# Sums of the activations made in SBUF after a copy out of PSUM, and block loads of the weights issued by GpSimd, in a one-core decoder block

## The chip, the cores and the metric

The kernel runs on one core of a Trainium2 chip. The metric is the device time of one execution in microseconds (us). Below, PE is TensorE's matmul stream and PEld its weight loads, DVE is VectorE, ACT is ScalarE, POOL is GpSimd, and SP is SyncE, which in this kernel mostly issues DMAs.

## The reference

One decoder layer over 256 rows of 2048 numbers, in fp32. Three attention-like mixers are merged through gates, and then comes the part that the change touches, a feed-forward block of width 8192:

```python
x = x + merged @ w_out[layer]
h2 = _rms(x, g_ffn_norm[layer])
x = x + jnp.square(jax.nn.relu(h2 @ w_ff_in[layer])) @ w_ff_out[layer]
```

## The kernel before, in words

Every weight is read from HBM once, as fp32. A tile `raw` is split into `whi` (an ACT cast, L187) and `wlo = raw - whi` (DVE, L188), the activations are split the same way into a high and a low half, and each product is made of three matmul passes: high by `whi`, low by `whi`, high by `wlo`. One pass over one k-tile (128 of the 2048 rows of a weight) is a matmul of 128x128 by 128x512. `split_into` (ACT L275, DVE L276) does the same split for all other tiles.

The feed-forward block runs in four quarters of 2048 hidden columns. A quarter first makes its hidden rows (`w_ff_in`), then adds their product with `w_ff_out` to the output. From the second half of quarter 0's `w_ff_out` on, the work is done in **units** (`unit`, L281) of 1024 columns: one unit in quarter 0, four in each later quarter (two of `w_ff_in`, then two of `w_ff_out`), 13 in all. In a unit, six of the 16 k-tiles go through a seven-product scheme of Strassen's kind over a 2x2 grid of blocks (two halves of the rows, two halves of the columns, two groups of three k-tiles). The other ten k-tiles are plain items, marked `n`. The order of a unit is fixed:

```python
UNIT = _order("B11", "n", "n", "n", "T2", "n", "T3", "n", "T1", "n", "B21", "n", "B22", "n", "T4", "n", "n")
```

Each letter item comes in two pieces, a of two k-tiles and b of one (`SUBS`), an `n` item is two k-tiles. The scheme needs two kinds of sums:

- **Sums of weight blocks** (`uload`). The four blocks B12, B11, B21 and B22 of a unit are loaded as tiles `sraw` of 768 KB (`fetch`, L203). DVE forms T3 = B22 - B12 (L216), T2 = B11 + T3 (L218), T1 (L222) and T4 (L230), each 128x1536. L216 needs the fourth block, which is asked for last. `fetch` for the next unit is called one block at a time, after items T2, T3, T1 and B21 of the current one. Before the change SP issues these loads, in one queue with the loads of `raw`.
- **Sums of the activations' blocks** (`sums_of`): four sums of the high/low input, split and kept in `sx` (of the normed input `x1T`, made once, from the SBUF tiles `xs`) or in `ss` (of a quarter's hidden rows, once per quarter, so four times). They are made in two pieces, of two k-tiles and of one.

`hidden_rows` makes the hidden rows: for each half of the rows four PE transposes put the squared ReLU `y` into a PSUM bank `tp` (L794), ACT and DVE split it into `hid` (L275, L276), and, before the change, `sums_of` reads both `tp` banks for its sums. It is a generator: `pump()` advances the queue `posts` (these rows) and the queue `attn` (side work) by one step after each item. For quarters 1 to 3 the second piece of `sums_of` falls between item `n` and item T3 of the quarter's second `w_ff_in` unit.

PSUM has four banks `acc`, two banks `sc` and two banks `tp`. The products B11 and T2 accumulate in `sc` banks; T3 and T1 take the two `tp` banks (name `pp`), the same that the transposes use. Every engine works through its instructions in a fixed order, which the compiler's scheduler sets from the program's order and the queues; `wahead` keeps the split of three items' weights ahead of PE, with four buffers each of `raw`, `whi` and `wlo` and six of `sraw`.

Of the kernel before, what the change touches and what calls it, by code (L numbers as in the profile page):

```python
# [11 lines left out]
F32 = mybir.dt.float32  # L12
F32R = mybir.dt.float32r
AF = mybir.ActivationFunctionType
ALU = mybir.AluOpType
# [3 lines left out]
P = 128  # L19
# [26 lines left out]
SH = 3  # L46
K1, K2 = [0, 1, 4], [2, 3, 5]
SUBS = [(0, 2), (2, 1)]
# [46 lines left out]
def tile_block(ctx: ExitStack, tc: tile.TileContext, io):  # L95
    nc = tc.nc
# [29 lines left out]
    posts, attn = deque(), deque()  # L126

    def step(queue):
        try:
            next(queue[0][1])  # L130
        except StopIteration:
            queue.popleft()
# [6 lines left out]
    def drain(queue, label):  # L139
        while any(l == label for l, _ in queue):  # L140
            step(queue)
# [26 lines left out]
    last_load = [None]  # L168
# [24 lines left out]
    def fetch(u, n):  # L193

        if u == len(units):
            return
        name, at = units[u]
        size = P * SH * 512
        got = ready.setdefault(u, {})
        for i, k in enumerate(list(BLOCKS)[len(got):n], len(got)):  # L200
            off = (at * len(BLOCKS) + i) * size
            got[k] = pool[0].tile([P, SH, 512], F32, tag="sraw", name="sraw")
            last_load[0] = nc.sync.dma_start(  # L203
                got[k], io[name][off:off + size].rearrange("(p g n) -> p g n", p=P, g=SH)).ins

    def uload(name, which):

# [64 lines left out]
    def split_into(hi, lo, src, scale=None):  # L272

        if scale is None:
            nc.scalar.copy(hi, src)  # L275
            nc.vector.tensor_tensor(lo, src, hi.bitcast(F32), op=ALU.subtract)  # L276
        else:
            nc.scalar.activation(hi, src, AF.Copy, scale=scale)  # L278
            nc.vector.scalar_tensor_tensor(lo, src, scale, hi.bitcast(F32), op0=ALU.mult, op1=ALU.subtract)

    def unit(name, sums, xh, xl, early, late):  # L281


# [359 lines left out]
    for t in range(2):  # L643
        nc.vector.scalar_tensor_tensor(zf[:, t, :], acc[t][:, 256:260], rstd[:, t:t + 1], bf,
                                       op0=ALU.mult, op1=ALU.add)
# [71 lines left out]
    ff = ctx.enter_context(tc.tile_pool(name="ff", bufs=1))  # L717
# [4 lines left out]
    for c in range(4):  # L722
# [6 lines left out]
        for j in range(2):  # L729
            tp = ps_tp.tile([P, 2, S], F32, tag="tp", name="tp")  # L730
# [18 lines left out]

    x1h, x1l = rows_of(x1T)  # L750

    S_USE = {"T1": 0, "T2": 1, "T3": 2, "B22": 3}

    def sums_of(a, ss):

        (a11, a12), (a21, a22) = a
        n = ss.shape[3]
        sf = ff.tile([P, 4, n, P], F32, tag="sf", name="sf", bufs=1)
        a21s = ff.tile([P, n, P], F32, tag="a21", name="a21s", bufs=1)
        nc.scalar.copy(a21s, a21)  # L760
        nc.vector.tensor_tensor(sf[:, 0], a22, a21s, op=ALU.add)  # L761
        nc.vector.tensor_tensor(sf[:, 2], a11, a21s, op=ALU.subtract)
        nc.vector.scalar_tensor_tensor(sf[:, 1], a11, -1.0, sf[:, 0], op0=ALU.mult, op1=ALU.add)
        nc.vector.tensor_tensor(sf[:, 3], a12, sf[:, 1], op=ALU.subtract)
        split_into(ss[:, 0], ss[:, 1], sf)

    def sums_for(at, ss):

        sums = {k: (lambda hl, g, i=i: ss[:, hl, i, g, :]) for k, i in S_USE.items()}
        sums["B11"] = lambda hl, g: at(K1[g], hl, slice(0, P))  # L770
# [4 lines left out]
    def partial_sums(p1, p6, p7, p5):  # L775
        p1s = ff.tile([P, 512], F32, tag="p1", name="p1s", bufs=1)
        uu = ff.tile([P, 2, 512], F32, tag="uu", name="uu", bufs=1)
        wz = ff.tile([P, 2, 512], F32, tag="wz", name="wz", bufs=1)
        nc.scalar.copy(p1s, p1)
        nc.vector.tensor_tensor(uu[:, 0, :], p6, p1s, op=ALU.add)  # L780
        nc.vector.tensor_tensor(uu[:, 1, :], p7, uu[:, 0, :], op=ALU.add)
        nc.vector.tensor_tensor(wz, p5[:, None, :].to_broadcast([P, 2, 512]), uu, op=ALU.add)
        return p1s, uu[:, 1, :], wz

    def hidden_rows(ys, hh, ss, wait):

        for _ in range(wait):
            yield
        tps = []
        for t in range(2):  # L790
            yield
            tp = ps_tp.tile([P, 4, P], F32, tag="tp", name="tp")
            for i in range(4):
                nc.tensor.transpose(tp[:, i, :], ys[t][:, i * P:(i + 1) * P], ident)  # L794
            ts = slice(t * P, (t + 1) * P)
            split_into(hh[:, :, 0, ts], hh[:, :, 1, ts], tp)
            tps.append(tp)
        if ss is not None:
            yield
            g0, n = SUBS[ss[1]]  # L800
            sums_of([[tp[:, n * i:n * i + n, :] for i in range(2)] for tp in tps], ss[0][:, :, :, g0:g0 + n, :])


    rrow = ff.tile([P, S], F32, name="rrow")
    sx = ff.tile([P, 2, 4, SH, P], F32R, name="sx")
# [16 lines left out]
            scaled.append(f)  # L822

    def split_rows():
        yield
        for g, f in enumerate(scaled):
            yield
            split_into(x1T[:, 4 * g:4 * g + 4, 0, :], x1T[:, 4 * g:4 * g + 4, 1, :], f)
            if g < len(SUBS):
                yield  # L830
                g0, n = SUBS[g]
                sums_of([[f[:, n * j:n * j + n, i * P:(i + 1) * P] for j in range(2)] for i in range(2)],
                        sx[:, :, :, g0:g0 + n, :])

    for q in range(4):
        hid = [ff.tile([P, 4, 2, S], F32R, tag="hid", name="hid", bufs=4) for _ in range(4)]
        ss = ff.tile([P, 2, 4, SH, P], F32R, tag="ss", name="ss", bufs=1)
        for sidx in range(4 if q == 0 else 0):
            if sidx == 1:
                attn.append(("x", scale_rows()))  # L840
            acc = strip_rows("w_ff_in", 512, KT, x1h, x1l)
            ys = []
            for t in range(2):
                y = ff.tile([P, 512], F32, tag="y", name="y", bufs=4)
                nc.scalar.activation(y, acc[t], AF.Relu, scale=ss2[:, t:t + 1])
                nc.scalar.activation(y, y, AF.Square)
                ys.append(y)
            posts.append(("h", hidden_rows(ys, hid[sidx], (ss, sidx) if sidx < len(SUBS) else None, 1)))
        for u in range(2 if q else 0):
            more = {}  # L850

            def early(*p):
                more[0, 0], more[0, 1], wz = partial_sums(*p)
                more[1, 0], more[1, 1] = wz[:, 0, :], wz[:, 1, :]

            def late(c, t, acc):
                y = ff.tile([P, 512], F32, tag="y", name="y", bufs=4)
                nc.vector.tensor_tensor(y, acc, more[c, t], op=ALU.add)
                nc.scalar.activation(y, y, AF.Relu)
                nc.scalar.activation(y, y, AF.Square)  # L860
                more["y", t] = y
                if t:
                    i = 2 * u + c
                    posts.append(("h", hidden_rows([more["y", 0], y], hid[i], (ss, i) if i < len(SUBS) else None,
                                                   0 if c else 2)))

            unit("w_ff_in", sums_for(lambda kt, hl, ts: x1T[:, kt, hl, ts], sx), x1h, x1l, early, late)
        if q == 0:
            drain(attn, "x")
            attn.append(("x", split_rows()))  # L870
        hidh = lambda kt, t: hid[kt // 4][:, kt % 4, 0, t * P:(t + 1) * P]
        hidl = lambda kt, t: hid[kt // 4][:, kt % 4, 1, t * P:(t + 1) * P]
        for c in range(0 if q else 2):
            acc = strip_rows("w_ff_out", 512, KT, hidh, hidl)
            cs = slice(c * 512, (c + 1) * 512)
            for t in range(2):
                nc.vector.tensor_tensor(x1[:, t, cs], acc[t], x1[:, t, cs], op=ALU.add)
        for u in range(0 if q else 1, 2):
            cols = [slice(1024 * u + 512 * c, 1024 * u + 512 * (c + 1)) for c in range(2)]

            def early(*p):
                p1s, u3, wz = partial_sums(*p)
                nc.vector.tensor_tensor(x1[:, 0, cols[0]], p1s, x1[:, 0, cols[0]], op=ALU.add)
                nc.vector.tensor_tensor(x1[:, 1, cols[0]], u3, x1[:, 1, cols[0]], op=ALU.add)
                nc.vector.tensor_tensor(x1[:, :, cols[1]], wz, x1[:, :, cols[1]], op=ALU.add)

            def late(c, t, acc):
                nc.vector.tensor_tensor(x1[:, t, cols[c]], acc, x1[:, t, cols[c]], op=ALU.add)  # L888
                if q == 3:
                    load(io["out"][t * P:(t + 1) * P, cols[c]], x1[:, t, cols[c]])  # L890

            unit("w_ff_out", sums_for(lambda kt, hl, ts: hid[kt // 4][:, kt % 4, hl, ts], ss), hidh, hidl, early, late)
        drain(attn, "x")
# [71 lines left out]
```

## Time and profile before

| | |
|---|---|
| time, median of 3 runs | 1412.69 us (1409.19, 1413.38, 1412.69) |
| profiled execution, its own time | 1411.21 us |
| span of the profiled execution (first to last instruction) | 1409.4 us |
| mean granted TensorE clock | 0.997 of 2.4 GHz |
| PE busy | 1393.0 us (99%) |
| DVE, ACT, POOL busy | 1024.9 us (73%), 759.9 us (54%), 37.5 us (3%) |
| HBM read | 271.31 MB, 194 GB/s over the span |

The profile is of one execution. Busy time counts the instructions of an engine; a matmul's end is modelled, and waits are put down to the last thing that was released. The span leaves out 1.8 us of the execution's own time.

### The profile page before, as it was taken

The page shows a single profiled execution, that of the slowest core. Times are in us where ns is not written, and L with a number is a line of the kernel's source. Part 1 is how long each engine was busy: PE and PEld are TensorE (multiplying, and loading weights), DVE is VectorE, ACT ScalarE, POOL GpSimd, SP SyncE. Part 2 cuts the span into 40 slices and gives each one's busy share as a digit, 9 for nine tenths or more (in the row PEclk, how much of TensorE's full clock was granted, in tenths as well). Part 3 has the DMA queues.
Part 4 walks back from the last instruction along what each step waited for, and adds up shares of the span by engine and source line. Part 5 has one row for each costly group of instructions (what it writes and reads, how often), then busy time and mean ns, then how long its engine had stood idle before and what let it go on. Part 6 is the DMA issues. An engine that isn't in the chain of part 4 may idle for free.

```text
span 1409.4 us, 17262 instructions
## 1 busy us (share of the span) xinstructions
PE 1393.0 (99%) x6343; PEld 1153.1 (82%) x6343; DVE 1024.9 (73%) x1167; ACT 759.9 (54%) x983; POOL 37.5 (3%) x41
## 2 busy tenths in 40 slices
PE   8999999999999999999999999999999999999998
PEld 6888888888888888888888888878888788887887
DVE  6647657566755646565567758899988899988996
ACT  7545545466444444444455635566555665556653
POOL 0211102000000000000000000000000000000000
PEclk9999999999999999999999999999999999999999
DMA  9747555655566666676675755655666556665562
GB/s 326 239 139 239 169 148 165 197 184 165 182 207 198 199 200 200 196 233 204 183 231 180 228 188 185 219 186 176 200 210 198 172 184 206 207 191 181 187 207 77
DMA packets 75524, 274.54 MB, mean 195 GB/s; under 512 B 8624, under 2 KB 9392, under 8 KB 75184
## 3 DMA queue, kind: packets, MB, share of 16 engines
q1 hardware_dynamic: 75296, 273.42, 60.6%
q8 instruction: 50, 0.82, 0.2%
q14 instruction: 34, 0.28, 0.1%
q10 hardware_dynamic: 144, 0.02, 0.0%
HBM read 271.31 MB, written 2.10 MB: 194 GB/s over the span
## 4 chain that ended last, share of the span: by engine, by line
PE 73%; DVE 0%; ACT 0%; issue 0%
PE acc L265 33%; PE acc L292 31%; PE pp L292 8%; PE tp L794 1%; PE tp L734 0%; PE tp L706 0%; DVE hid L276 0%; ACT hid L275 0%; DVE sf L761 0%; ACT a21s L760 0%; DVE x L888 0%; PE rr L813 0%
## 5 line engine op out<-in xcount | busy, mean ns | idle before, releaser
L188 DVE TENSOR_TENSOR wlo<-raw,whi 128x1024 fp32r<-128x1024 f32 (+2 forms) x425 | 509.6, 1204 | 283.1 <-ACT whi L187 274.2
L187 ACT CAST whi<-raw 128x1024 fp32r<-128x1024 f32 (+2 forms) x425 | 441.3, 1039 | 455.9 <-PE acc L265 313.7
L265 PE MATMUL acc<-whi,xT 128*128 128x512 f32 (+1 forms) x1472 | 393.6, 389 | 5.7 <-ACT xT L278 5.4
L265 PEld LDWEIGHTS acc<-whi,xT 128*128 128x128 f32 x1472 | 272.7, 189 | 61.5 <-ACT xT L278 6.1
L265 PE MATMUL acc<-wlo,xT 128*128 128x512 f32 (+1 forms) x736 | 226.2, 388 | 0.0
L275 ACT CAST whi<-sraw 128x1024 fp32r<-128x1024 f32 (+1 forms) x182 | 151.0, 837 | 115.3 <-PE acc L292 83.4
L276 DVE TENSOR_TENSOR wlo<-sraw,whi 128x1024 fp32r<-128x1024 f32 (+1 forms) x182 | 169.8, 953 | 22.2 <-ACT whi L275 16.4
L292 PE MATMUL acc<-whi,hid 128*128 128x512 f32 x644 | 166.4, 391 | 0.0
L265 PEld LDWEIGHTS acc<-wlo,xT 128*128 128x128 f32 x736 | 136.9, 188 | 28.1 <-issue 1.0
L292 PE MATMUL acc<-whi,x1T 128*128 128x512 f32 x552 | 140.7, 391 | 0.0
L292 PEld LDWEIGHTS acc<-whi,hid 128*128 128x128 f32 x644 | 120.3, 188 | 24.5
L292 PEld LDWEIGHTS acc<-whi,x1T 128*128 128x128 f32 x552 | 103.2, 188 | 21.2
L292 PE MATMUL acc<-wlo,hid 128*128 128x512 f32 x322 | 91.1, 390 | 0.0
L292 PE MATMUL acc<-wlo,x1T 128*128 128x512 f32 x276 | 76.9, 390 | 0.0
L292 PEld LDWEIGHTS acc<-wlo,hid 128*128 128x128 f32 x322 | 60.2, 188 | 12.4
L265 PE MATMUL acc<-whi,x1T 128*128 128x512 f32 x256 | 70.0, 394 | 0.0
L265 PE MATMUL acc<-whi,mT 128*128 128x512 f32 x256 | 69.9, 392 | 0.0
L265 PE MATMUL acc<-whi,oT 128*128 128x512 f32 x224 | 60.0, 390 | 0.6 <-ACT oT L278 0.6
L292 PEld LDWEIGHTS acc<-wlo,x1T 128*128 128x128 f32 x276 | 51.6, 188 | 10.6
L265 PEld LDWEIGHTS acc<-whi,mT 128*128 128x128 f32 x256 | 47.9, 188 | 9.6
L265 PEld LDWEIGHTS acc<-whi,x1T 128*128 128x128 f32 x256 | 47.5, 188 | 9.4
L265 PEld LDWEIGHTS acc<-whi,oT 128*128 128x128 f32 x224 | 42.0, 188 | 9.6 <-ACT oT L278 0.9
(201 smaller groups left out, 1337.5 us busy)
## 6 DMA issues: line engine op xcount, KB each, us to landing
raw<-in_w_gate_dram SPq DMA_DIRECT2D x96, 512.0 KB, 3.6
raw<-in_w_ff_in_dram SPq DMA_DIRECT2D x92, 512.0 KB, 4.1
raw<-in_w_ff_out_dram SPq DMA_DIRECT2D x86, 512.0 KB, 4.3
raw<-in_w_proj_dram SPq DMA_DIRECT2D x77, 512.0 KB, 3.9
sraw<-in_w_ff_out_blocks_dram SPq DMA_DIRECT2D x28, 768.0 KB, 4.5
sraw<-in_w_ff_in_blocks_dram SPq DMA_DIRECT2D x24, 768.0 KB, 5.5
raw<-in_w_out_dram SPq DMA_DIRECT2D x32, 512.0 KB, 3.5
raw<-in_w_up_c_dram SPq DMA_DIRECT2D x12, 512.0 KB, 3.5
```

Source lines behind the costliest of these rows:

```text
L187: nc.scalar.copy(hi[:, gs, :], raw[:, gs, :])
L188: nc.vector.tensor_tensor(lo[:, gs, :], raw[:, gs, :], hi[:, gs, :].bitcast(F32), op=ALU.subtract)
L265: nc.tensor.matmul(acc[t][:, :n], lhsT=xs(kt, t), rhs=ws[:, g, :], start=(first and kt == 0), stop=(last and kt == nkt - 1),)
L275: nc.scalar.copy(hi, src)
L276: nc.vector.tensor_tensor(lo, src, hi.bitcast(F32), op=ALU.subtract)
L292: nc.tensor.matmul(acc, lhsT=x(hl, g), rhs=w[:, g, :], start=(first and i == 0 and g == 0), stop=(last and i == 2 and g == n - 1))
L794: nc.tensor.transpose(tp[:, i, :], ys[t][:, i * P:(i + 1) * P], ident)
```

## The change

Two edits, and a third that follows from them.

1. The block loads in `fetch` are issued by GpSimd in place of SP, and no longer note themselves as the last load (to which later small loads are tied).
2. The activations' blocks are copied out of PSUM by ACT right after the transposes (`keep`, into a tile `sf` of SBUF), and `sums_of` becomes a step by step generator that runs later, in the `attn` queue, in place in `sf`, for all three k-tiles at once. The copy `a21s` and the scalar form of the second sum are gone. `drain(attn, "s")` makes sure that the sums are written before the quarter's `w_ff_out` starts.
3. `hidden_rows` is a step shorter for the rows that carry sums, so what follows it in `posts` comes a step earlier, and the scheduler's order moves around it.

```diff
@@ fetch
             got[k] = pool[0].tile([P, SH, 512], F32, tag="sraw", name="sraw")
-            last_load[0] = nc.sync.dma_start(
-                got[k], io[name][off:off + size].rearrange("(p g n) -> p g n", p=P, g=SH)).ins
+            nc.gpsimd.dma_start(got[k], io[name][off:off + size].rearrange("(p g n) -> p g n", p=P, g=SH))
@@ sums
-    S_USE = {"T1": 0, "T2": 1, "T3": 2, "B22": 3}
-
-    def sums_of(a, ss):
-
-        (a11, a12), (a21, a22) = a
-        n = ss.shape[3]
-        sf = ff.tile([P, 4, n, P], F32, tag="sf", name="sf", bufs=1)
-        a21s = ff.tile([P, n, P], F32, tag="a21", name="a21s", bufs=1)
-        nc.scalar.copy(a21s, a21)
-        nc.vector.tensor_tensor(sf[:, 0], a22, a21s, op=ALU.add)
-        nc.vector.tensor_tensor(sf[:, 2], a11, a21s, op=ALU.subtract)
-        nc.vector.scalar_tensor_tensor(sf[:, 1], a11, -1.0, sf[:, 0], op0=ALU.mult, op1=ALU.add)
-        nc.vector.tensor_tensor(sf[:, 3], a12, sf[:, 1], op=ALU.subtract)
-        split_into(ss[:, 0], ss[:, 1], sf)
+    S_USE = {"T3": 0, "T2": 1, "T1": 2, "B22": 3}
+
+    def sums_of(sf, ss):
+
+        def op(dst, a, b, how):
+            nc.vector.tensor_tensor(sf[:, dst], sf[:, a], sf[:, b], op=how)
+
+        yield
+        op(2, 0, 2, ALU.add)
+        op(0, 1, 0, ALU.subtract)
+        yield
+        op(1, 2, 1, ALU.subtract)
+        op(3, 3, 1, ALU.subtract)
+        yield
+        nc.scalar.copy(ss[:, 0], sf)
+        yield
+        nc.vector.tensor_tensor(ss[:, 1], sf, ss[:, 0].bitcast(F32), op=ALU.subtract)
+
+    def keep(sf, i, t, src):
+
+        g0, n = SUBS[i]
+        nc.scalar.copy(sf[:, 1 - t::2, g0:g0 + n, :], src.rearrange("p (h g) n -> p h g n", h=2))
@@ hidden_rows
-            tps.append(tp)
-        if ss is not None:
-            yield
-            g0, n = SUBS[ss[1]]
-            sums_of([[tp[:, n * i:n * i + n, :] for i in range(2)] for tp in tps], ss[0][:, :, :, g0:g0 + n, :])
+            if sf is not None:
+                keep(sf[0], sf[1], t, tp[:, :2 * SUBS[sf[1]][1], :])
+                if t and sf[1] == len(SUBS) - 1:
+                    attn.append(("s", sums_of(sf[0], sf[2])))
@@ split_rows (the sums sx of the input)
             if g < len(SUBS):
-                yield
-                g0, n = SUBS[g]
-                sums_of([[f[:, n * j:n * j + n, i * P:(i + 1) * P] for j in range(2)] for i in range(2)],
-                        sx[:, :, :, g0:g0 + n, :])
+                for t in range(2):
+                    keep(sfx, g, t, f[:, :2 * SUBS[g][1], t * P:(t + 1) * P])
+        yield from sums_of(sfx, sx)
@@ loop over the quarters
             attn.append(("x", split_rows()))
+        drain(attn, "s")
```

How the order of instructions moves is shown at three places. In such rows a bracket lists the engines or queues that the instruction waits for (DMAHW a transfer issued by SP, DMASW one issued by GpSimd), and x3 stands for three more of the same.

PE, around item T3 of the second `w_ff_in` unit of quarters 1 to 3 (the same in all three). `tp<-ident,y` are the transposes of the second half of the hidden rows, `acc<-whi,x1T` and `acc<-wlo,x1T` plain matmuls, `pp<-whi,sx` the first product of T3. Before:

```order
L292 MATMUL acc<-whi,x1T 128x512 [waits Activation_49]
L292 MATMUL acc<-whi,x1T 128x512 x7
L292 MATMUL acc<-wlo,x1T 128x512 [waits DVE_49]
L292 MATMUL acc<-wlo,x1T 128x512 x3
L794 MATMUL tp<-ident,y 128x128 [waits DVE_49]
L794 MATMUL tp<-ident,y 128x128 x3
L292 MATMUL pp<-whi,sx 128x512 [waits DVE_49,PE_49]
```

and now:

```order
L800 MATMUL tp<-ident,y 128x128 [waits PE_49,Activation_49]
L800 MATMUL tp<-ident,y 128x128 x3
L291 MATMUL acc<-whi,x1T 128x512 [waits Activation_49]
L291 MATMUL acc<-whi,x1T 128x512 x7
L291 MATMUL acc<-wlo,x1T 128x512 [waits DVE_49]
L291 MATMUL acc<-wlo,x1T 128x512 x3
L291 MATMUL pp<-whi,sx 128x512 [waits PE_49,Activation_49]
```

The transposes stood right ahead of T3's first product; now twelve plain matmuls stand between them, and the product waits for ACT where it waited for DVE.

DVE, around the sum T3 = B22 - B12 of a unit (before L216, now L215; the place shown is the third unit). `wlo<-sraw,whi` is the low half of a block's piece, `wlo<-raw,whi` that of an `n` item, `wz<-pp,uu` belongs to the products. Before:

```order
L782 TENSOR_TENSOR wz<-pp,uu 128x1024 [waits DVE_49,PE_49]
L188 TENSOR_TENSOR wlo<-raw,whi 128x1024 [waits DMAHW6_49,Activation_49]
L276 TENSOR_TENSOR wlo<-sraw,whi 128x1024 [waits PE_49,Activation_49]
L216 TENSOR_TENSOR sraw<-sraw 128x1536 [waits DMAHW4_49,DMAHW1_49]
L276 TENSOR_TENSOR wlo<-sraw,whi 128x512 [waits PE_49,Activation_49]
L188 TENSOR_TENSOR wlo<-raw,whi 128x1024 [waits DMAHW7_49,PE_49,Activation_49]
L218 TENSOR_TENSOR sraw<-sraw 128x1536 [waits DMAHW0_49,DVE_49]
```

and now:

```order
L789 TENSOR_TENSOR wz<-pp,uu 128x1024 [waits DVE_49,PE_49]
L188 TENSOR_TENSOR wlo<-raw,whi 128x1024 [waits DMAHW5_49,Activation_49]
L275 TENSOR_TENSOR wlo<-sraw,whi 128x1024 [waits PE_49,Activation_49]
L275 TENSOR_TENSOR wlo<-sraw,whi 128x512 [waits PE_49,Activation_49]
L215 TENSOR_TENSOR sraw<-sraw 128x1536 [waits DMASW3_49,DMASW0_49]
L188 TENSOR_TENSOR wlo<-raw,whi 128x1024 [waits DMAHW6_49,PE_49,Activation_49]
L217 TENSOR_TENSOR sraw<-sraw 128x1536 [waits DMASW1_49,DVE_49]
```

The split of the 512-column piece went from behind the sum to ahead of it, and the sum waits for transfers issued by GpSimd.

PE, where the `w_ff_in` part of quarters 1 to 3 ends and `w_ff_out` begins. `pp<-whi,hid` and `acc<-whi,hid` are the first matmuls of `w_ff_out`; the transposes need the sums `y` of the last `acc<-wlo,x1T` passes (two matmuls each for the four pairs of column half and row half, the pair of the transposes shown first). Before:

```order
L292 MATMUL acc<-wlo,x1T 128x512 [waits DVE_49]
L292 MATMUL acc<-wlo,x1T 128x512 x3
L292 MATMUL pp<-whi,hid 128x512 [waits Activation_49]
L292 MATMUL pp<-whi,hid 128x512 x3
...
L292 MATMUL acc<-wlo,hid 128x512 [waits DVE_49]
L292 MATMUL acc<-wlo,hid 128x512 x3
L292 MATMUL acc<-whi,hid 128x512 [waits DVE_49,Activation_49]
L292 MATMUL acc<-whi,hid 128x512 x3
L794 MATMUL tp<-ident,y 128x128 [waits Activation_49]
```

and now:

```order
L291 MATMUL pp<-whi,hid 128x512 [waits Activation_49]
L291 MATMUL pp<-whi,hid 128x512 x3
L291 MATMUL acc<-wlo,x1T 128x512 [waits DVE_49]
L291 MATMUL acc<-wlo,x1T 128x512 x3
L291 MATMUL acc<-wlo,x1T 128x512 [waits DVE_49]
L291 MATMUL acc<-wlo,x1T 128x512 x3
L291 MATMUL pp<-wlo,hid 128x512 [waits DVE_49]
L291 MATMUL pp<-wlo,hid 128x512
L291 MATMUL pp<-whi,hid 128x512 [waits Activation_49]
...
L291 MATMUL acc<-whi,hid 128x512 [waits DVE_49,Activation_49]
L291 MATMUL acc<-whi,hid 128x512 x3
L800 MATMUL tp<-ident,y 128x128 [waits Activation_49]
```

Between the last matmul that the first transposes' `y` needs and the transposes stood 26 matmuls in quarters 2 and 3 (32 in quarter 1); now it is 15 in all three.

SP issues 52 loads fewer (its rows fall from 198 to 102), POOL issues these 52, all behind its last small operation.

## Rows read from the trace of the kernel before

**Rows 1.** Part 1 of the page, busy time of each engine.

```profile
PE 1393.0 (99%) x6343; PEld 1153.1 (82%) x6343; DVE 1024.9 (73%) x1167; ACT 759.9 (54%) x983; POOL 37.5 (3%) x41
```

**Rows 2.** Waits of PE: us in total, times, longest.

```profile
PE pp L292 <- DVE sf L761: 6.3, 3, 2.1
```

**Rows 3.** The chain of waits from 943.88: start us, us, what.

```profile
943.88 2.77 PE acc L292 x12
946.65 0.45 PE tp L794 x4
...
947.12 0.59 ACT hid L275
...
947.74 0.70 DVE hid L276
...
948.47 0.27 ACT a21s L760
...
948.76 0.30 DVE sf L761
```

**Rows 4.** Groups by line, forms together: count, busy us, mean ns, idle before.

```profile
L761 DVE TENSOR_TENSOR sf<-tp,a21s 128x256 f32<-128x256 f32 (+1 forms) x8 | 2.8, 354 | 1.3 <-ACT a21s L760 1.3
L276 DVE TENSOR_TENSOR ss<-sf,ss 128x1024 fp32r<-128x1024 f32 (+1 forms) x8 | 7.6, 952 | 2.1 <-ACT ss L275 2.1
L275 ACT CAST ss<-sf 128x1024 fp32r<-128x1024 f32 (+1 forms) x8 | 6.7, 834 | 3.2 <-DVE sf L764 3.2
```

**Rows 5.** Groups by line, each form apart: the nearest operations to the new ones.

```profile
L764 DVE TENSOR_TENSOR sf<-tp,sf 128x256 f32<-128x256 f32 x4 | 1.7, 417 | 0.0
L764 DVE TENSOR_TENSOR sf<-tp,sf 128x128 f32<-128x128 f32 x4 | 1.2, 292 | 0.1
L218 DVE TENSOR_TENSOR sraw<-sraw 128x1536 f32<-128x1536 f32 x13 | 22.8, 1751 | 0.0
L275 ACT CAST ss<-sf 128x1024 fp32r<-128x1024 f32 x4 | 4.2, 1050 | 0.0
L760 ACT COPY a21s<-tp 128x256 f32<-128x256 f32 x4 | 1.5, 366 | 0.8 <-DVE hid L276 0.8
L779 ACT COPY p1s<-pp 128x512 f32<-128x512 f32 x13 | 7.5, 574 | 0.0
```

**Rows 6.** Stretch of one unit: PE, PEld, DVE, ACT, POOL busy, clock, DMA share, GB/s.

```profile
943.00:986.00 43.00, 40.88 (x188) 33.68 (x188) 40.53 (x46) 28.62 (x39) 0.00 (x0) 1.00 0.57 187
```

**Rows 7.** The weight sum T3 by line: idle time before it and its releasers.

```profile
L216 DVE TENSOR_TENSOR sraw<-sraw 128x1536 f32<-128x1536 f32 x13 | 22.9, 1758 | 16.8 <-DMA sraw<-in_w_ff_in_blocks_dram 10.3 <-DMA sraw<-in_w_ff_out_blocks_dram 6.5
```

**Rows 8.** Timeline of the third unit: start us, us, engine, what, [idle before <-releaser].

```profile
908.06 0.33 SPq L203 DMA_DIRECT2D sraw<-in_w_ff_in_blocks_dram  x1
...
914.76 1.76 DVE L216 TENSOR_TENSOR sraw<-sraw 128x1536 f32<-128x1536 f32 x1 [2.82 <-DMA sraw<-in_w_ff_in_blocks_dram]
...
916.44 0.69 DVE L276 TENSOR_TENSOR wlo<-sraw,whi 128x512 fp32r<-128x512 f32 x1
...
917.82 0.39 PE L292 MATMUL acc<-wlo,sx 128*128 128x512 f32 x1
...
919.85 1.82 DVE L276 TENSOR_TENSOR wlo<-sraw,whi 128x1024 fp32r<-128x1024 f32 x2
...
921.67 0.62 PE L292 MATMUL acc<-wlo,x1T 128*128 128x512 f32 x2
```

**Rows 9.** Block loads: the tile's view, and part 6 of the page (median to landing).

```profile
DMA to landing us min/median/max: 4.1/4.8/8.8
...
sraw<-in_w_ff_in_blocks_dram SPq DMA_DIRECT2D x24, 768.0 KB, 5.5
```

**Rows 10.** POOL's own small operations, by line.

```profile
L379 POOL TENSOR_SCALAR ss<-ss 128x4 f32<-128x4 f32 (+1 forms) x16 | 13.4, 836 | 281.8 <-DVE ss L391 170.8 <-DVE ss L506 111.0
```

**Rows 11.** From a unit's last pass to its rows `y`, by line and form.

```profile
L858 DVE TENSOR_TENSOR y<-acc,p1s 128x512 f32<-128x512 f32 x6 | 4.1, 684 | 0.2 <-PE acc L292 0.2
L859 ACT ACTIVATE y<-y 128x512 f32<-128x512 f32 x24 | 14.4, 625 | 1.6 <-DVE y L858 1.6
```

More of the change, by code (lines that the diff above doesn't have):

```diff
@@ L783, in partial_sums, with hidden_rows @@
         return p1s, uu[:, 1, :], wz
-    def hidden_rows(ys, hh, ss, wait):
+    def hidden_rows(ys, hh, sf, wait):
         for _ in range(wait):
             yield
-        tps = []
         for t in range(2):
@@ L824, in split_rows @@
     def split_rows():
+        sfx = ff.tile([P, 4, SH, P], F32, tag="sf", name="sf", bufs=1)
         yield
@@ L837, in tile_block @@
         ss = ff.tile([P, 2, 4, SH, P], F32R, tag="ss", name="ss", bufs=1)
+        sf = ff.tile([P, 4, SH, P], F32, tag="sf", name="sf", bufs=1)
         for sidx in range(4 if q == 0 else 0):
@@ L847, in tile_block @@
                 ys.append(y)
-            posts.append(("h", hidden_rows(ys, hid[sidx], (ss, sidx) if sidx < len(SUBS) else None, 1)))
+            posts.append(("h", hidden_rows(ys, hid[sidx], (sf, sidx, ss) if sidx < len(SUBS) else None, 1)))
         for u in range(2 if q else 0):
@@ L863, in late @@
                     i = 2 * u + c
-                    posts.append(("h", hidden_rows([more["y", 0], y], hid[i], (ss, i) if i < len(SUBS) else None,
+                    posts.append(("h", hidden_rows([more["y", 0], y], hid[i], (sf, i, ss) if i < len(SUBS) else None,
                                                    0 if c else 2)))
```

## The prediction

> **What bounds the kernel now.** I read the busy times first. PE works 1393.0 of the 1409.4 us span [rows 1], so no change that leaves PE its matmuls can take more than the 16 us in which it stands still, and this one leaves them: the same passes run before and after. Then the waits of PE: the only one in the feed-forward part is that of T3's first product, which waits three times for DVE's sum at L761, 6.3 us in all and at most 2.1 us at once [rows 2]. The chain of waits around one of the three shows what happens [rows 3]: the transposes end, ACT casts `hid` for 0.59 us, DVE makes its low half in 0.70, ACT copies `a21s` in 0.27, DVE reads the other block out of PSUM in 0.30, and only then is the bank free for the product. The whole chain stands open, because the transposes are the last thing ahead of the product in PE's order. Last I read who is nearly late. In the stretch of such a unit DVE is busy 40.53 of 43 us, ACT 28.62 [rows 6]: DVE is the second bound of the feed-forward part, and its only long idle time there is in front of L216, which waits for the fourth block load in each of the 13 units, 16.8 us in all [rows 7]. These waits are hidden today, but not by much, as worked out below.
>
> **The three stalls at T3: -6.3 us.** In the new order twelve plain matmuls stand between the last transposes and the product. Such a run of twelve takes 2.77 us [rows 3]. What the bank waits for is now the cast (0.59), DVE's low half (0.70) and beside that ACT's copy of 256 or 512 columns (0.37 or 0.57 [rows 5]): some 1.3 to 1.4 us with the hand-overs. The cover exceeds it by 1.4 us, enough for one ACT cast of 1024 columns (1.05 [rows 5]) that happens to stand in front. So the 6.3 us go. If cover is missing by a cast and a DVE operation together, each of the three would keep some 0.8 us.
>
> **The sums themselves: 0.** Before, a set of sums costs DVE 2.8 us in four groups of short operations (eight pieces for four sets: L761 shows 2.8 us for eight, the other three lines the same within 0.1) and 1.9 for the low half (7.6 by four) [rows 4]. After, it is four operations on 384 columns and one on 1536. 128 columns take 0.292 and 256 take 0.417 [rows 5], so 384 should take 0.54, four 2.2; 1536 columns take 1.75 [rows 5]. That is 3.9 in place of 4.7: 0.8 us less for DVE, five times (four quarters and the input). ACT before: two copies (0.37 and 0.27) and 1.7 of casts per set, 2.3 [rows 3, 4, 5]. After: two copies of 512 and two of 256 columns, 1.9, and a cast of 1536, at most one and a half times 1.05, 1.6 [rows 5]: 3.5, so 1.2 us more, five times. Neither is on PE's path: ACT has a third of its time free [rows 6], and DVE gets lighter. I cost both at nothing; without that cover the sum over five sets would be +6 us for ACT, -4 for DVE. The five sets fall at other places of their units than before, which I price with the third term.
>
> **The block loads move to POOL: 0, and this is the weak point.** SP needs 0.33 us to issue one [rows 8], and it lands 4.1 us after its issue at best, 4.8 in the median [rows 9]. The trace has no DMA issued by POOL, so the price is bounded. Below: nothing. An earlier landing would gain nothing either, since no wait of PE ends on a transfer [rows 2]; SP, freed of 52 issues, can run its other loads sooner, and PE doesn't wait for these. Above: a small operation of POOL (0.84 [rows 10]), plus one DVE operation of 1536 columns that holds the issue up (1.75 [rows 5]), plus 1.4 for sharing the DMA engines with the loads of `raw`, which no longer stand in one line with the blocks (5.5 in the median against 4.1 at best [rows 9]): 4.0 us in all. I take 0.8, one small POOL operation ahead of an otherwise equal path, since that is the one row of the engine that will issue.
>
> What does a late landing cost? L216 ends DVE's idle time at the landing, so all that stands behind it on DVE slides by the same amount, and PE waits for the low halves among it. In the third unit, with its wait of 2.82 us the tightest, the split behind L216 ends at 917.13 and PE uses it at 917.82: 0.69 us of cover [rows 8]. That split now stands ahead of the sum, in the idle time, so it no longer counts and takes its 0.69 us of work out of what follows. Next is the 1024-column split of the pair that starts at 919.85: the pair ends at 921.67, its second piece takes 0.69, so the first is ready at about 921.0, and PE uses it at 921.67 [rows 8]. 0.6 to 0.7 of cover and 0.69 moved ahead make 1.3 us. The other twelve sums wait 1.2 us in the mean ((16.8 - 2.82) / 12 [rows 7, 8]), 1.6 less than this one; where the sum starts nearer to its turn, DVE has lost less to the wait. I credit them with a third of that, 0.5 us, as further cover: 1.8. That share is my choice. So a delay of 0.8 is hidden everywhere; the cost begins at 1.3 in one unit and, from about 1.8, grows by the excess in each of the twelve units whose blocks are loaded while the unit before runs.
>
> Here the Trainium skill speaks against the change. Its page "SBUF — State Buffer", section "SBUF: two separate sides", says that GpSimd itself writes the descriptors of the DMAs it issues, and can't while DVE runs an operation in a mode that takes their shared port. DVE's two-input fp32 operations show no fast mode here: 128 more columns cost 0.125 us, about 1 ns a column [rows 5]; so by the page's narrow wording nothing is held, and the sum stays as it is. The Trainium skill's page "DMA: Bandwidth & Descriptors", section "Specifications", gives about 1 us to the first byte from GpSimd's queue and 0.6 from sync's: an estimate of +0.4 us by it, which leaves the sum the same.
>
> **The transposes at the start of `w_ff_out`: +1.5 us.** The shorter `hidden_rows` brings them forward. Between the last matmul of the pass that ends their `y` and the transposes now stand 15 matmuls, 3.5 us at 2.77 for twelve [rows 3], where 26 or more stood (6.0). The chain between is DVE's sum (0.68), and two activations on ACT (0.63 each) [rows 11]: 1.9 to 2.1 with hand-overs. 1.4 us are spare. One cast on ACT (1.05 [rows 5]) in front of an activation fits; a cast and a 1024-column operation on DVE (about 1.2, the first of the pair in [rows 8]) don't: 0.9 late. With a busy DVE I take 0.5 us for each of the three, between 0 and 0.9.
>
> **The sum.** -6.3 + 0 + 0 + 1.5 = -4.8 us on the profiled execution's own 1411.2, which is 1406.4. The median of the runs shown stands 1.5 us above that execution, so against it I forecast 1412.7 - 4.8 = 1407.9. About 0.3%, 4.2 us, is what a measurement of this kernel can tell from no change: faster ends at 1408.5 and slower begins at 1416.9.
>
> **Rivals.**
> *No new wait at all.* The transposes find their rows ready: -6.3, 1406.4. For it speaks the 1.4 us of spare time, against it DVE at 94% of the unit [rows 6]. Chance 0.13.
> *The gain is eaten.* The block loads land some 1.9 to 2.5 us later: an excess of 0.1 to 0.7 us in twelve units gives back 1.2 to 8.4 us, so 1409 to 1416. Chance 0.20.
> *Slower: the loads of POOL land late.* The issue is held until DVE is between operations, or the transfers share with the `raw` loads; either puts 1.4 to 1.8 us on top of the 0.84. At 3.0 us the price is 12 x (3.0 - 1.8) = 14.4, the sum +9.6, 1422. It decides from a delay of 2.55 us, where 12 x 0.75 = 9.0 turns -4.8 into +4.2. For it: DVE has little idle time to leave [rows 6], and the wait at L216 already ends last on DVE [rows 7]. Against: it takes two of the three parts of the upper bound at once. Chance 0.25. This is also what the skill's page on SBUF would give if its lock held for every DVE operation with two inputs; no row here shows that it does.
> *The change doesn't do what it says.* The bank is still held when the product comes, now by ACT's copy behind other casts: each stall keeps most of its 2.1 us and the time stays near 1412. Against it stand the twelve matmuls. Chance 0.04.
>
> **How the numbers follow.** My forecast has 0.38, of which 0.30 lies below 1408.5 (its own range is 1406 to 1410). Faster: 0.30 + 0.13 = 0.43. Same: 0.08 + 0.20 + 0.04 = 0.32. Slower: 0.25. The range runs from 1404, some 2 us under the case without waits for the spread of the runs, to 1421, which leaves out the slower half of the slow case, 0.12, and some 0.05 at the low end.
>
> **What the profile after would show.** The wait of `pp` on L761 is gone and nothing takes its place there; ACT's copies take about 0.57 and 0.37 us; DVE's busy time is about 4 us less and ACT's 6 us more. The block loads' time to landing in the new trace, minus the 4.8 us of before, is the delay: under 1.3 confirms the forecast. Wrong in either direction shows as waits of PE for `wlo` (L188 or L275) in units, behind the T3 sum, or for `y` at the transposes. A wait for `ss` at the first product of `w_ff_out`'s T2 would mean that the sums come too late, which I priced at nothing.

## The result, and the profile after

The changed kernel takes 1401.68 us (median of 4 runs, 1401.09 to 1402.17) against 1411.15 for the kernel before (4 runs, 1409.19 to 1413.38): a ratio of 0.9932, 95% interval 0.9914 to 0.9951. That is 9.5 us less. The forecast was 4.8 less (1407.9 from a median of 1412.7 over the three runs then known), and its range, 1404 to 1421, lies wholly above the result. The sign was right, the size half of what came.

The profiled executions differ by 9.1 us (spans of 1409.4 and 1400.3), and the head of the page after says in two numbers where from:

```profile
span 1400.3 us, 17290 instructions
...
PE 1390.3 (99%) x6343; PEld 1151.3 (82%) x6343; DVE 1021.3 (73%) x1142; ACT 761.4 (54%) x988; POOL 65.7 (5%) x93
```

PE's idle time fell from 1409.4 - 1393.0 = 16.4 us [rows 1] to 1400.3 - 1390.3 = 10.0, which is 6.4: the stalls. Its busy time fell by 2.7 us, with the same 6343 instructions. 6.4 + 2.7 = 9.1. So the same matmuls took less time in sum, and the forecast has no term for that.

The waits of PE after, in total, times and longest, show that no wait in the feed-forward part is left; both lines are of the kernel's first third, and were there before:

```profile
PE acc L264 <- ACT xT L277: 5.4, 2, 4.8
PE acc L264 <- ACT oT L277: 0.6, 1, 0.6
```

The chain of waits at T3, the place of [rows 3], is PE alone now. Twelve plain matmuls follow the last transposes, and the product of T3 starts behind them without a gap:

```profile
943.13 0.44 PE tp L800 x4
943.57 0.94 PE acc L291 x4
944.50 0.43 PE tp L800 x4
944.94 2.76 PE acc L291 x12
947.70 4.08 PE pp L291 x18
```

What became of the busy time is found with the granted clock. Stretches of 2 us of the kernel before, around the second of its three stalls, with busy time of PE, PEld, DVE, ACT and POOL, the granted clock, the DMA share and GB/s:

```profile
1116.00:1118.00 2.00, 2.00 (x10) 1.62 (x9) 2.00 (x4) 1.62 (x3) 0.00 (x0) 1.00 1.01 357
1118.00:1120.00 2.00, 1.18 (x8) 0.76 (x6) 1.95 (x4) 1.12 (x2) 0.00 (x0) 1.00 0.53 209
1120.00:1122.00 2.00, 0.71 (x2) 0.65 (x3) 1.50 (x5) 0.37 (x2) 0.00 (x0) 0.85 0.59 157
1122.00:1124.00 2.00, 2.00 (x6) 1.52 (x6) 0.69 (x1) 1.25 (x2) 0.00 (x0) 0.50 0.57 237
1124.00:1126.00 2.00, 2.00 (x9) 1.60 (x8) 0.79 (x2) 1.34 (x2) 0.00 (x0) 0.79 0.00 0
1126.00:1128.00 2.00, 2.00 (x11) 1.65 (x10) 2.00 (x2) 1.57 (x3) 0.00 (x0) 1.00 0.00 0
```

PE stands still for 2.1 us, and just behind its restart at 1121.29 the clock falls to 0.50, which is 1.2 GHz in place of 2.4: six matmuls are on record in 1122 to 1124 where ten to twelve are in a full stretch. Then the clock is back. The four matmuls that open T3's product show it in their times, here and in the changed kernel (start us, us, engine, what):

```profile
1121.29 1.94 PE L292 MATMUL pp<-whi,sx 128*128 128x512 f32 x4 [2.12 <-DVE sf L761]
```

```profile
947.53 1.07 PE L291 MATMUL pp<-whi,sx 128*128 128x512 f32 x4
```

The loss is 2 x (0.15 + 0.50 + 0.21) = 1.7 us, and it lies under running matmuls, so it counts as busy time. The third stall (1292.9) shows the same, the first (947.1) stays at 1.00. In the changed kernel the three places are at 1.00 throughout. Two such stretches are 3.4 us, more than the 2.7 by which the busy time fell. The rest is at the other end of the execution: the changed kernel's began more slowly. Two matmuls from the first microseconds and two after 30 us, before and then after:

```profile
8.80 0.63 PE L265 MATMUL acc<-wlo,xT 128*128 128x512 f32 x2
...
30.60 0.62 PE L265 MATMUL acc<-wlo,xT 128*128 128x512 f32 x2
```

```profile
8.90 1.05 PE L264 MATMUL acc<-wlo,xT 128*128 128x512 f32 x2
...
31.24 0.62 PE L264 MATMUL acc<-wlo,xT 128*128 128x512 f32 x2
```

The first hundred matmuls, the same in both kernels, took 24.9 us of PE's time before and 25.9 after, and 25.3 to 26.4 in the profiles of experiments 1 to 4. The pair's 1.05 us is what a pair takes in the stretch at 0.50 (the one at 1123.03 in the kernel before), but the column of the granted clock reads 1.00 at the start; why the start differs is not shown. Behind the start the sum closes better: from PE's 4001st matmul to its last, which holds every place where its order changed, PE takes 531.3 us before and 521.5 after. Of these 9.9 us, 6.3 are idle time and 3.6 busy time, against 3.4 for the clock.

The runs of before agree. Over 19 further runs, those with a mean granted clock of 0.998 or 0.999 took 1409.2 to 1410.2 us (9 runs), those with 0.997 took 1410.6 and 1410.8, and those with 0.996 took 1413.0 to 1414.0 (8 runs). As an estimate from these numbers, one, two or three stalls with a slow stretch of 1.7 us behind them, on 1401.7 + 6.3, give 1409.7, 1411.4 and 1413.1; the traces show only executions with two. The changed kernel's runs all show 1.00 and lie within 1.1 us.

The new operations cost what the nearest rows had said [rows 5]. Groups by line and form, with busy us and mean ns:

```profile
L772 ACT COPY sf<-tp 128x512 f32<-128x512 f32 x8 | 4.7, 583 | 1.0 <-DVE hid L275 1.0
L772 ACT COPY sf<-tp 128x256 f32<-128x256 f32 x8 | 3.0, 369 | 4.1 <-DVE hid L275 4.1
L756 DVE TENSOR_TENSOR sf<-sf 128x384 f32<-128x384 f32 x20 | 11.1, 556 | 1.7 <-ACT sf L772 1.4
L767 DVE TENSOR_TENSOR ss<-sf,ss 128x1536 fp32r<-128x1536 f32 x4 | 7.0, 1756 | 0.2 <-ACT ss L765 0.2
L765 ACT CAST ss<-sf 128x1536 fp32r<-128x1536 f32 x4 | 5.9, 1472 | 0.0
```

And the block loads on POOL, the weak point of the forecast: the view of the tile `sraw` (duration of an issue in ns, min/median/max, and the time to landing), and the waits of the sum T3.

```profile
L203 POOL DMA_DIRECT2D sraw<-in_w_ff_out_blocks_dram x28: 537/537/723, 716.7 to 1336.7; - x28
L203 POOL DMA_DIRECT2D sraw<-in_w_ff_in_blocks_dram x24: 537/537/542, 807.1 to 1248.7; - x24
...
DMA to landing us min/median/max: 4.3/4.6/8.3
```

```profile
DVE sraw L215 <- DMA sraw<-in_w_ff_in_blocks_dram: 5.5, 4, 2.0
DVE sraw L215 <- DMA sraw<-in_w_ff_out_blocks_dram: 5.0, 4, 1.7
```

An issue takes 0.54 us against SP's 0.33 [rows 8], the best landing is 0.2 us later, the median 0.2 earlier than in [rows 9]. The sum T3 waits 10.5 us in all, eight times, where it waited 16.8 in thirteen [rows 7].

### The profile page after: what moved, and what is told of

It reads as the page before. It is cut to its first block, busy times and chain, and to the rows that moved or that the text cites. A ratio compares the mean times of both kernels' runs of the same rounds, so it can differ in the third digit from the quotient of the medians.

```text
span 1400.3 us, 17290 instructions
## 1 busy us (share of the span) xinstructions
PE 1390.3 (99%) x6343; PEld 1151.3 (82%) x6343; DVE 1021.3 (73%) x1142; ACT 761.4 (54%) x988; POOL 65.7 (5%) x93
## 4 chain that ended last, share of the span: by engine, by line
PE 73%; DMA 0%; DVE 0%; ACT 0%; DVEq 0%; issue 0%; ACTq 0%
PE acc L264 33%; PE acc L291 30%; PE pp L291 7%; PE tp L800 1%; DMA raw<-in_w_ff_out_dram 0%; PE tp L705 0%; PE tp L733 0%; DVE wlo L188 0%; ACT whi L187 0%; DVE sraw L217 0%; DVE x L895 0%; ACT y L866 0%; DVEq L968 0%; ACT y L865 0%; PE rr L818 0%
## 5 line engine op out<-in xcount | busy, mean ns | idle before, releaser
L291 PE MATMUL acc<-wlo,hid 128*128 128x512 f32 x322 | 88.2, 390 | 0.0
```

The costliest lines, as they stand in the source:

```text
L291: nc.tensor.matmul(acc, lhsT=x(hl, g), rhs=w[:, g, :], start=(first and i == 0 and g == 0), stop=(last and i == 2 and g == n - 1))
```

## The experiments

The theory after the result: the whole gain comes from the PSUM banks. The old sums read the two `tp` banks late, the scheduler therefore puts the last transposes right ahead of T3's product, PE stands still, and most of the stalls drag the clock down behind them. The rival: a part of the gain, some 3 to 4 us, comes from the GpSimd queue, which takes 52 loads out of SP's line. Experiments 1 to 4 ran on one chip with 19 runs of before (median 1410.58, 1409.21 to 1413.97), 5 and 6 on one chip with nine (median 1413.02, 1409.49 to 1413.43).

**1. The new sums with the loads back on SP.**

```diff
-            nc.gpsimd.dma_start(got[k], io[name][off:off + size].rearrange("(p g n) -> p g n", p=P, g=SH))
+            last_load[0] = nc.sync.dma_start(
+                got[k], io[name][off:off + size].rearrange("(p g n) -> p g n", p=P, g=SH)).ins
```

> The new sums with the block loads back on SP. If the gain is the three stalls at T3 and the low clock that follows two of them, both from PSUM banks held too long, the time is that of the changed kernel within 0.15%, 1400 to 1404 us, no wait of PE in the feed-forward part, granted clock 1.00. If part of the gain is GpSimd's queue (SP relieved, blocks earlier), 3 to 4 us come back: 1404.5 to 1406.

1402.44 us (1402.05 to 1402.85, 6 runs), ratio to before 0.9933 (0.9919 to 0.9947): the ratio of the changed kernel, to 0.0001. PE is busy 1390.4 us, and its only waits are the two of the first third. The rival's 3 to 4 us don't come back. Beside experiment 4, on the same chip, this kernel is 0.8 us longer, with ranges that overlap.

**2. The old sums with the loads on GpSimd.** The edit is that of the change in `fetch`, alone.

> The old sums with the block loads on GpSimd. By the first theory the three stalls of 2.1 us stay and the time is that of before, 1409 to 1413 us. By the other, 3 to 4 us are gained without touching the sums: 1406 to 1408.

1411.54 us (1409.07 to 1413.68, 12 runs), ratio 1.0001 (0.9989 to 1.0012). The queue by itself shows no effect, and the interval leaves room for 1.7 us at most either way. The waits and the stretches around two of the stalls show both the stall and the clock behind it:

```profile
PE pp L291 <- DVE sf L760: 6.3, 3, 2.1
```

```profile
944.00:952.00 8.00, 5.88 (x28) 4.63 (x27) 6.91 (x12) 4.87 (x8) 0.54 (x1) 0.95 0.71 228
952.00:960.00 8.00, 8.00 (x31) 6.49 (x30) 6.18 (x8) 4.73 (x6) 0.54 (x1) 0.84 0.54 172
...
1126.00:1134.00 8.00, 8.00 (x31) 6.41 (x31) 6.25 (x7) 4.39 (x6) 0.54 (x1) 0.83 0.46 144
```

Here it is the first and the second stall that lower the clock, and the third that doesn't: which one is spared differs between the two profiles.

**3. The stalls filled with matmuls that add nothing.** The kernel before, with nine matmuls by a tile of zeros behind the last transposes; six plain matmuls come to stand behind them as well.

```diff
+                if what == ("T3", 0) and fill[0]:
+                    with tc.issue_after(last_tp[0]):
+                        for i in range(fill[0]):
+                            nc.tensor.matmul(r[0, 0], lhsT=zero, rhs=ws[0][:, i % n, :], start=False, stop=False)
...
+            fill[0] = 9 * u
             unit("w_ff_in", sums_for(...
```

> The kernel before with nine more matmuls by a tile of zeros (they add nothing to the result) between the last transposes and T3's product in quarters 1 to 3; six plain matmuls move there with them. PE has 27 matmuls more, 6.2 us, and no stall of 2.1 us. If the stalls cost their 6.3 us alone, the two cancel and the time stays at 1411 us. If the low clock after a stall belongs to the stall, it goes too: granted clock 1.00 throughout and 1407 to 1408.5 us, though PE does more.

1406.86 us (1406.75 to 1408.05, 8 runs), ratio 0.9965 (0.9953 to 0.9977). PE does 27 matmuls more, and the kernel is 3.7 us quicker than before. At 0.23 us each [rows 3] they are worth 6.2 us and PE's idle time falls by as much, from 16.4 to 10.2, so the 3.7 are the clock's. In the profile PE's busy time rises by 3.1 us only, to 1396.1, where the zeros alone would add 6.2:

```profile
PE 1396.1 (99%) x6370; PEld 1156.9 (82%) x6370; DVE 1023.6 (73%) x1168; ACT 757.7 (54%) x983; POOL 37.5 (3%) x41
```

The same stretch as the second one above:

```profile
1118.00:1120.00 2.00, 2.00 (x12) 1.69 (x11) 2.00 (x4) 0.72 (x2) 0.00 (x0) 1.00 0.78 268
1120.00:1122.00 2.00, 2.00 (x11) 1.64 (x10) 1.08 (x4) 0.78 (x2) 0.00 (x0) 1.00 0.00 0
1122.00:1124.00 2.00, 2.00 (x11) 1.65 (x10) 0.97 (x3) 1.32 (x3) 0.00 (x0) 1.00 0.31 37
```

Take the 6.2 us of zeros off, and 1400.7 is left, within 1 us of the changed kernel. This run carries the study: without the standstill the low clock is gone (1.00 from 20 us to PE's last matmul at 1402), though the four transposes are still there, and its price comes on top of the stall's own.

**4. The sums made at once.** What the change puts in the later queue is run right behind the copies.

```diff
-                    attn.append(("s", sums_of(sf[0], sf[2])))
+                    for _ in sums_of(sf[0], sf[2]):
+                        pass
```

> The changed kernel, but the sums are made at once after the copies, not in the later queue. If the copy out of PSUM is what frees the bank, nothing changes: 1400 to 1404 us, no stall at T3. If it matters that the sums run later, DVE's four sums and the wide split stand in front of something that PE waits for, and 2 to 6 us come back.

1401.63 us (1400.64 to 1402.80, 6 runs), ratio 0.9927 (0.9913 to 0.9942). It doesn't matter when the sums run. PE's rows are the same, row by row, as in the changed kernel: the scheduler had put them where it wanted. The orders of two more kernels, which were not run, say the same of the generator's shorter wait: taking the step before `sums_of` out of the old kernel leaves PE's rows as they were, and putting it back into the new one does too. So neither the queue nor the step moves the transposes; what is left of the edit that touches a bank is the copy that frees it, though no run has the copy alone. The addresses of the tiles in the built kernels show one thing more that no view of the profile tells: T3's product took the bank of the second half's transposes, whose last reader is L761, and takes the bank of the first half's now, in all three quarters.

**5 and 6. What if the loads did land late?** The weak point of the forecast was a price per late landing. Two kernels make the fourth block of the changed kernel late: by a small transfer into the same tile that the load must wait for, and by loading the block twice.

```diff
+            if k == "B22":
+                nc.gpsimd.dma_start(got[k][:, 0, 0:64], io[name][off:off + P * 64].rearrange("(p n) -> p n", p=P))
             nc.gpsimd.dma_start(got[k], io[name][off:off + size]...
```

```diff
-            nc.gpsimd.dma_start(got[k], io[name][off:off + size]...
+            for _ in range(2 if k == "B22" else 1):
+                nc.gpsimd.dma_start(got[k], io[name][off:off + size]...
```

> The changed kernel with a small transfer (128x64) into the fourth block's tile ahead of its load; the load waits for it, so the sum T3 of each unit is later by the small transfer's landing, about 2 us. By the prediction's rule (cover 1.8 us in the mean, then twelve times the excess) the cost is 2 to 5 us: 1404 to 1407. If the cover behind the sum is larger than I worked out, nothing: 1400.5 to 1403.

> The changed kernel with the fourth block loaded twice into the same tile, the second load waiting for the first: the sum T3 is later by a whole landing, about 4.5 us. By the prediction's rule 12 x (4.5 - 1.8) = 32 us: about 1434. If the cover is larger by 2 us, some 8 us: about 1410. A granted clock below 1.00 after stalls adds to either.

The small one takes 1404.29 us (1403.74 to 1405.00, 4 runs), 2.6 more than the changed kernel; the small transfer lands after 2.0 us at best. That is inside the rule's 2 to 5. (The changed kernel did not run beside these two; before's runs span the same times on both chips, so I compare the times.) The double one takes 1417.43 (1416.22 to 1418.40, 6 runs), 15.7 more, where the rule gave 32. The sum T3 waits for its blocks 17.8 us in the first and 35.7 in the second, against 10.5. The waits of PE in the second are mostly not for low halves of weights, which show only as ten short waits of PEld (2.9 us in all), but for banks and rows that a late DVE hands back:

```profile
PE acc L292 <- DVE x L896: 6.4, 5, 1.7
...
PE acc L292 <- DVE y L865: 3.4, 4, 1.1
PE acc L292 <- ACT whi L275: 1.0, 1, 1.0
```

So cover was there, and the slope behind it was too steep: the delays differ by about 2.5 us (4.5 and 2.0), and (15.7 - 2.6) / 2.5 is 5 us for each us of delay, not 12. Drawn back to no cost, that line gives a cover of about 1.5 us, near the forecast's 1.3 to 1.8. This is an estimate from two points, with two cautions: the scheduler knew of the delays and laid both kernels out anew, so these are not the changed kernel's order with a late transfer, and the double load also moves 13 blocks of 768 KB more.

## Why the prediction was wrong

**The three stalls, -6.3: right.** PE's idle time fell by 6.4 us, the wait on L761 is gone, twelve matmuls of 2.76 us cover it. The spare was less than the 1.4 us I gave it: DVE made the two low halves of `hid` behind a split of 1.23 us, the copy that frees the first half's bank ends at 946.83, and the product starts at 947.53, 0.7 later:

```profile
945.74 1.28 DVE L275 TENSOR_TENSOR hid<-tp,hid 128x512 fp32r<-128x512 f32 x2
...
946.46 0.37 ACT L772 COPY sf<-tp 128x256 f32<-128x256 f32 x1 [0.89 <-DVE hid L275]
```

One detail of the cause was wrong as well: "The shorter `hidden_rows` brings them forward", I wrote of the transposes at the start of `w_ff_out`. The two orders beside experiment 4 show that the shorter generator moves none of PE's rows.

**The clock: a term that was missing.** This is the step that failed. The opening of the forecast bounds the gain by the time in which PE stands still and takes its busy time as fixed ("this one leaves them"). It wasn't: 3.4 us of the 1393.0 were lost to the clock in the same matmuls behind two of the stalls; with the slower start of the later execution, 2.7 of them show in the busy times. The notice was in my own table, a mean granted clock of 0.997: 0.003 of 1409 us is 4 us, 3.4 of it in the two stretches and the rest behind PE's last matmul, where the clock is down again. I read the stall's stretch in the chain and not in a view with the clock. The spread of the three runs shown, 4.2 us, was a second hint. The trace shows 0.50 at 1122 to 1124, behind a standstill of 2.1 us. The Trainium skill, page "TensorE: Matmul & The Clock Gate", section "Part 1: The HAM clock gate (the "warmup" mystery)", gives a PE that has been idle 1.2 GHz and a busy one 2.4; the trace agrees on the two levels, 0.50 and 1.00.

**The transposes at the start of `w_ff_out`, +1.5: mis-sized.** It measured 0.1, one gap of 0.08 us. The chain was as tight as feared, and just fits. Timeline of the changed kernel (start us, us, engine, what), from the sum to the transposes:

```profile
971.08 0.69 DVE L864 TENSOR_TENSOR y<-acc,p1s 128x512 f32<-128x512 f32 x1 [1.11 <-PE acc L291]
...
971.97 1.06 ACT L187 CAST whi<-raw 128x1024 fp32r<-128x1024 f32 x1 [1.19 <-PE acc L291]
...
972.92 0.63 ACT L865 ACTIVATE y<-y 128x512 f32<-128x512 f32 x1
...
973.59 0.63 ACT L866 ACTIVATE y<-y 128x512 f32<-128x512 f32 x1
...
974.28 0.65 PE L800 MATMUL tp<-ident,y 128*128 128x128 f32 x4
```

The one ACT cast in front that I had said fits is there, and the square ends 0.06 us before the transposes start. The DVE operation that would have made it late isn't: DVE waits for PE at that place, 1.11 us, though it is busy nine tenths of the unit. I had taken the share of a whole unit for the state at one place.

**The block loads, 0: right, for a better reason.** The price per load was 0.2 us at best landing, not 0.8, so no cover was used, and experiments 1 and 2 put the queue's effect below what they resolve (0.9933 beside 0.9932, and 1.0001, each to about 0.0013). The rival in which DVE holds the issues up found nothing: the issue takes 0.537 us in the median and 0.72 at most while DVE is busy 39 of the 43 us of a unit (936 to 979). This is where the Trainium skill's page "SBUF — State Buffer", section "SBUF: two separate sides", by its narrow wording let the loads pass, and the trace agrees. The price that this rival used, twelve times the excess, was, by the estimate above, more than twice too steep (experiments 5 and 6).

**The sums, 0: right.** DVE's busy time fell by 3.6 us (forecast 4). ACT's rose by 1.5, though the new rows account for the forecast 5 to 6; where the rest of it was saved I did not follow, since ACT ends no wait of PE in the feed-forward part.

The corrected sum is -6.3 (stalls) - 3.4 (clock) + 0.1 (transposes) + 0 + 0 = -9.6 us, against the 9.9 measured from the 4001st matmul on; 0.3 stay open. The slower start and the end give 0.6 and 0.2 back, which makes the -9.1 of the two spans. Of the 4.3 us by which the forecast missed these, the clock less the slower start is 2.7, the transposes are 1.4.

## What to carry to other kernels

Where PE is the bound and stands still for a couple of microseconds, look at the granted clock of the stretch behind it before pricing the stall: here three stalls of 2.1 us cost 6.3 themselves and 3.4 more in matmuls slowed behind two of them, and a mean clock of 0.997 or a spread of the runs that the code doesn't explain is the sign. A PSUM bank that is shared between transposes and products was here best emptied by one copy at once; what was then made of the copy, and when, made no difference. Before pricing a wait by how busy an engine is on average, look at the place: DVE, 90% busy, was idle where it mattered.

## What was not expected of the hardware

Not every stall lowers the clock. Of three alike, 2.1 us long and behind the same four transposes, two did in the profile of before (the second and third) and two in that of experiment 2 (the first and second). The fall came 0.1 and 0.5 us after PE's restart in the first and 1.0 and 1.4 us after it in the other. In experiment 6 PE waits five times for L896, up to 1.7 us; its profile keeps 1.00 until PE's work is done, and its runs a mean granted clock of 0.998 to 1.000. What sets apart the stalls that lower the clock is not shown. Loads issued by GpSimd landed after 4.6 us in the median against SP's 4.8, with an issue of 0.54 us against 0.33, and the kernel's time shows no difference.
